# Storing attention outputs already split: a two-layer encoder trunk on one core

## The chip, the core and the metric

The kernel runs on one core of a Trainium2 chip. A core has TensorE (PE in the profile, with its weight loads as PEld), VectorE (DVE), ScalarE (ACT), GpSimd (POOL) and SyncE (SP), each with its own instruction stream, in order. SP issues all of this kernel's DMAs, on one queue that 16 DMA engines serve. The metric is device time in microseconds of one execution; before the change it is 2732.51 us, the median of 3 runs (2729.88 to 2735.3).

## The reference: what is computed

One inference step of a streaming encoder with two layers, for a prompt (1024 positions) and 8 samples of 16 positions, which stand together as 1152 rows (nine tiles of 128, the last one all samples).

```
for l in range(DEPTH):                                   # 2
    sh_m, sc_m, g_m, sh_f, sc_f, g_f = split(silu(c) @ w_ada[l] + b_ada[l], 6)
    h = x * (1 + sc_m) + sh_m
    # layer 0: window attention (128 back, 16 heads, 4 key heads, sinks, T5 bias)
    # layer 1: band attention (8 chunks of 64 back, 16 heads, clipped relative bias), shared K/V
    o = softmax(q @ k.T * 0.125 + bias) @ v
    x = layer_norm(ALPHA * x + (1 + g_m) * (o @ w_o[l]), ln_g[l, 0], ln_b[l, 0])
    f = (gelu(conv3(h2 @ w_up)[g]) * conv3(h2 @ w_up)[a]) @ w_down[l]
    x = layer_norm(ALPHA * x + (1 + g_f) * f, ln_g[l, 1], ln_b[l, 1])
```

Everything is float32. A matrix product is made with three products of halves: each operand is split into a high part (cast to the rounded format fp32r) and a low part (the rest), and hi*lo, lo*hi and hi*hi are added up. So each operand of a large product stands twice, as `hi` and `lo`, and a *split* is one cast (mostly on ScalarE, `L183`) and one subtraction (on POOL or VectorE, `L194`).

## The kernel before

The tensor `H` (128 partitions, 2 parts, 8 chunks of 128 channels, 1152 rows) holds the left operand of each projection, both parts. In attention it holds the input of the query projections; once the last query block (`qblock`, at `L313`) has read it, it is filled again with the attention outputs, which the output projection (`mmX`, `L326`) reads.

Attention goes through 8 pairs of heads `c`, each with two heads `a`, each head with two halves `h` of 512 queries; a half is two steps of the loop over `work` (64 steps). Step by step the loop issues scores (`L558`, `L561`), the row minimum with the bias (`L525`), the exponential (`L529`), transposes (`L587`) with a split of the probabilities (`L593`, `L594`), and some steps later `finish`: `values` multiplies with V (`L609`), adds the two partial results into the buffer `on` (`L622`, `L623`), and `normalise` loads the reciprocal row sums into `rb` (`L644`) and multiplies on POOL (`L647`). The biases are loaded at `L537`, two heads deep, and their corners are set by POOL (`L538`, `L539`).

`on` has room for one pair of heads. For the pairs 0 to 5 each normalised half is stored to DRAM, `oN` (`L649`). The pairs 6 and 7 are split straight into `H`. After the last query block the loop loads the stored pairs back into the low part of `H` (`oload`, `L659`, steps 51 to 55 by the table `OAT`), and casts them there: `ocast`, `L664`, steps 52 to 58 by the table `CAT`, one ScalarE cast and one POOL subtraction in place for each pair and one for the first half of the samples' outputs.

Beside this run the 16 *items*, the samples' attention (`L701`, `L727`, `L736`, `L749`, with cache loads such as `L689`), in the steps of `ITEMS`; the adaLN products of layer 0 (`L240`, weights loaded at `L232`) as background work; and the loads of the output projection's weights (`WAT`).

`out_proj` then takes the tiles in the order 8, 0, 1, ... 7. A tile's two halves go to PSUM banks 0 to 3 in turn, and VectorE evicts each by a product with the gate row (`L1122`): `gateS`, one row for each sample, for tile 8, and `gateP` for the others. These tables and the two rows of the layer norm come from `ln_consts`: four loads (`L971` gateP, `L972` gateS, `L979` twice), which the code orders behind the last load of reciprocals (`issue_after(self.lastdma)`). In the arena `F`, `gateS` has columns 6396 to 7420, which during attention belong to the samples' queries and the first score buffer.

A planner orders each engine's instructions: it runs the program in a model of the chip and takes, on each engine, the instruction that is ready there and earliest in the program.

Of the kernel before, what the change touches and what calls it, by code (L numbers as in the profile page):

```python
# [10 lines left out]
F32 = mybir.dt.float32  # L11
# [4 lines left out]
D = 1024  # L16
# [31 lines left out]
OAT = {51: (0, 1, 2), 52: (3,), 53: (4,), 54: (5,), 55: (6,)}  # L48
CAT = {52: 0, 53: 1, 54: 2, 55: 3, 56: 4, 57: 5, 58: 6}
WAT = {52: 0, 54: 1, 56: 3, 59: 2}  # L50
# [55 lines left out]
class Trunk:  # L106
    def __init__(self, ctx, tc, I, O):
# [4 lines left out]
        nc = self.nc  # L112
# [280 lines left out]
    def attention(self, l, wk):  # L393
        nc, I = self.nc, self.I
# [245 lines left out]
        def normalise(c, a, h):  # L640
            r = slice(64 * a, 64 * a + 64)
            q = slice(h * 512, h * 512 + 512)
            src = self.rD[l][2 * c + a : 2 * c + a + 1, q]
            st = nc.sync.dma_start(rb[r, :], bass.AP(src.tensor, src.offset, [[0, 64], [1, 512]]))  # L644
# [8 lines left out]
        def oview(c):  # L653
            if c < 6:
                return [self.H[:, i, c, 0:1024] for i in range(2)]
            return [self.H[:, i, 0:4, 1024:1152] for i in range(2)]

        def oload(c):
            nc.sync.dma_start(oview(c)[1].bitcast(F32), self.oN[c] if c < 6 else self.oSD.rearrange("c p t -> p c t"))  # L659
# [127 lines left out]
        def finish(k):  # L787
            x = halves[k]
            values(x)
            if x.h:  # L790
# [17 lines left out]
        for i, x in enumerate(work):  # L808
            scores(x)
            k = i // 2  # L810
# [134 lines left out]
    def ln_region(self):  # L945
# [18 lines left out]
    def ln_consts(self, l, i):  # L964
        self.ln_gates(l, i)
        self.ln_rows(l, i)

    def ln_gates(self, l, i):
        nc = self.nc
        g = self.gd[2 * l + i]  # L970
        nc.sync.dma_start(self.gateP, bass.AP(g.tensor, g.offset, [[0, 128], [1, D]]))  # L971
        nc.sync.dma_start(self.gateS, bass.AP(g.tensor, g.offset + D, [[D, 8], [0, 16], [1, D]]))  # L972

# [120 lines left out]
    def out_proj(self, l, xsrc, xdst, aff):  # L1094
# [985 lines left out]
```

## Time and profile before

| | us |
|---|---|
| median of 3 runs | 2732.51 (2729.88 to 2735.3) |
| the profiled execution | 2728.86 |
| its span in the trace | 2727.1 |
| TensorE busy | 2627.6 (96%) |
| VectorE busy | 1936.6 (71%) |
| ScalarE busy | 1346.0 (49%) |
| POOL busy | 1067.1 (39%) |
| DMA | 498.29 MB, 55.4% of 16 engines' span |

An engine's busy time is the sum of its instructions' times. In a row such as `L183 ACT CAST H<-F ... x2 | 1.2, 611 | 0.0` stand the line of the kernel, the engine, the operation, what it writes and reads, how often, then the busy us, the mean ns of one, and the engine's idle time before them. In a timeline, the first numbers are start and duration in us, and brackets tell how long the engine had been idle and what ended that. In a view of stretches the share of the DMA engines comes last but one and can be a little over 1 where packets overlap.

### The profile page before, as it was taken

To read this page: it belongs to the slowest core of one execution; us is meant where nothing else is said; L and a number is where in the kernel's file an instruction comes from. 1 tells how busy PE (TensorE), PEld (TensorE's weight loads), DVE (VectorE), ACT (ScalarE), POOL (GpSimd) and SP (SyncE) were. 2 spreads that over 40 slices of the span, in tenths; PEclk is the share of its full clock that TensorE was granted. 3 is DMA by queue.
4 is the path that set the end of the run, shared out by engine and by line. 5 is a ranking of instruction groups with operands and counts; after the bars stand their busy time and mean duration, and the time that the engine had idled before them with its cause. 6 is when DMAs were issued, how large, how long until landed. Compare 5 with 4: busy or idle time off the path is not lost. (4 is left out here: it accounts for less than half of the span.)

```text
span 2727.1 us, 47308 instructions
## 1 busy us (share of the span) xinstructions
PE 2627.6 (96%) x17394; PEld 2343.4 (86%) x17394; DVE 1936.6 (71%) x3846; ACT 1346.0 (49%) x2777; POOL 1067.1 (39%) x771
## 2 busy tenths in 40 slices
PE   7999889999999999999999999989999999999997
PEld 6997768989999998888898888867899999998786
DVE  4376768876677675767764677777888777878668
ACT  3475733533343344444446666672445454556553
POOL 3032523444344447675220121242467666552101
PEclk9999999999999999999999999999999999999999
DMA  8656534644443447666658457783444334349673
GB/s 321 207 156 197 155 110 166 219 172 140 149 149 138 152 140 240 222 224 218 232 198 279 142 151 199 197 255 131 170 153 174 139 126 146 118 145 297 220 240 124
DMA packets 229384, 498.29 MB, mean 183 GB/s; under 512 B 37440, under 2 KB 98960, under 8 KB 229152
## 3 DMA queue, kind: packets, MB, share of 16 engines
q1 hardware_dynamic: 229152, 495.27, 55.4%
q8 instruction: 137, 2.24, 0.4%
q14 instruction: 95, 0.78, 0.1%
HBM read 378.15 MB, written 126.47 MB: 185 GB/s over the span
## 5 line engine op out<-in xcount | busy, mean ns | idle before, releaser
L1237 PE MATMUL PS<-H,wh 128*128 128x256 f32 (+1 forms) x2304 | 353.8, 295 | 0.0
L1237 PEld LDWEIGHTS PS<-H,wh 128*128 128x128 f32 x2304 | 321.0, 189 | 0.0
L1197 DVE TENSOR_TENSOR F<-PS,F 128x256 f32<-128x256 f32 (+1 forms) x446 | 196.8, 451 | 159.5 <-PE PS L1237 153.4
L183 ACT CAST wh<-F 128x512 fp32r<-128x512 f32 (+3 forms) x221 | 135.5, 625 | 197.6 <-PE PS L1237 91.5
L194 DVE TENSOR_TENSOR wl<-F,wh 128x512 fp32r<-128x512 f32 (+2 forms) x205 | 198.3, 978 | 43.3 <-ACT wh L183 42.9
L1237 PE MATMUL PS<-H,wl 128*128 128x320 f32 (+1 forms) x1152 | 201.9, 296 | 4.9 <-DVE wl L194 2.6
L1237 PE MATMUL PS<-xa,wh 128*128 128x320 f32 (+1 forms) x1168 | 178.9, 294 | 0.0
L1237 PEld LDWEIGHTS PS<-H,wl 128*128 128x128 f32 x1152 | 169.2, 189 | 11.2 <-issue 5.1
L1237 PEld LDWEIGHTS PS<-xa,wh 128*128 128x128 f32 x1168 | 162.3, 189 | 0.0
L647 POOL TENSOR_TENSOR F<-F,x2r 64x512 f32<-64x512 f32 x62 | 79.2, 1278 | 208.1 <-DVE F L623 186.4
L1495 DVE TENSOR_TENSOR xa<-xa 128x384 fp32r<-128x384 f32 x66 | 100.5, 1535 | 77.5 <-ACT xa L183 64.3
L183 ACT CAST wh<-ws 128x512 fp32r<-128x512 f32 (+1 forms) x123 | 90.8, 744 | 114.5 <-PE PS L1237 49.9
L1357 POOL TENSOR_TENSOR F<-F 128x1152 f32<-128x1152 f32 x44 | 124.6, 2833 | 44.2 <-DVE F L1350 24.4
L313 PE MATMUL PS<-H,w0r 128*128 128x384 f32 (+1 forms) x720 | 137.0, 340 | 0.0
L1286 DVE SCALAR_TENSOR_TENSOR F<-F 128x1024 f32<-128x1024 f32 (+2 forms) x160 | 132.5, 878 | 4.8 <-ACT F L1325 4.0
L525 DVE CUSTOM_DVE_ANT_0 F<-PS,F,C 128x256 f32<-128x256 f32 (+3 forms) x208 | 97.2, 479 | 50.8 <-PE PS L561 25.1
L326 PE MATMUL PS<-xa,H 128*128 128x512 f32 x504 | 128.2, 395 | 5.2 <-ACT xa L183 3.3
L313 PE MATMUL PS<-H,wh 128*128 128x384 f32 (+1 forms) x672 | 132.8, 339 | 0.0
L313 PEld LDWEIGHTS PS<-H,w0r 128*128 128x128 f32 x720 | 124.6, 188 | 1.6 <-DVE F L633 0.4
L326 PE MATMUL PS<-wh,H 128*128 128x512 f32 (+1 forms) x468 | 118.0, 360 | 0.7 <-ACT wh L183 0.5
L587 PE MATMUL PS<-C,F 128*128 128x128 f32 x720 | 111.6, 279 | 6.9 <-DVE C L636 3.1
L313 PEld LDWEIGHTS PS<-H,wh 128*128 128x128 f32 x672 | 117.1, 188 | 0.5 <-issue 0.2
(361 smaller groups left out, 6917.0 us busy)
## 6 DMA issues: line engine op xcount, KB each, us to landing
ws<-in_adaw_dram SPq DMA_DIRECT2D x63, 512.0 KB
ws<-in_wup_dram SPq DMA_DIRECT2D x51, 512.0 KB
F<-in_adaw_dram SPq DMA_DIRECT2D x49, 512.0 KB
actD<-F SPq DMA_DIRECT2D x33, 576.0 KB
F<-in_wup_dram SPq DMA_DIRECT2D x37, 512.0 KB
ws<-in_wdn_dram SPq DMA_DIRECT2D x33, 512.0 KB
F<-in_wdn_dram SPq DMA_DIRECT2D x33, 512.0 KB
xa<-kH SPq DMA_DIRECT2D x60, 256.0 KB
```

What stands on the lines that cost most here:

```text
L183: nc.scalar.copy(out, in_)
L194: self.eng(el).tensor_sub(lo, src, hi.bitcast(F32))
L313: mm = self.nc.tensor.matmul(out[:, 0:n], w[a][:, k * 128 : k * 128 + 128], H[:, p, k, s0 : s0 + n], start=i == 0, stop=i == 23)
L326: self.nc.tensor.matmul(out[:, 0:n], H[:, p, j * kn + k, t0 : t0 + 128], w[a][:, k * n : k * n + n], start=i == 0, stop=i == 23,)
L525: nc.vector.tensor_tensor_reduce(out=p[:, c0 : c0 + w], in0=ps, in1=b, scale=1.0, scalar=init, op0=ALU.add, op1=ALU.min, accum_out=nm)
L587: nc.tensor.transpose(t[:, n * 128 : n * 128 + 128], p[:, (kt - k0) * 128 : (kt - k0) * 128 + 128], self.ident)
L647: self.eng("v" if last else "p").tensor_mul(on[r, q], on[r, q], rb[r, :])
L1197: nc.vector.tensor_add(d, v(ps), a if len(a.shape) == 3 else v(a))
L1237: self.pairmm = nc.tensor.matmul(ps[:, 0:m], w[a][:, k * 128 : k * 128 + 128], x(p, k, n), start=start and c == 0, stop=c == 11, skip_grou ...
L1286: nc.vector.scalar_tensor_tensor(o, u, cw[:, cc, i : i + 1], o, op0=ALU.mult, op1=ALU.add)
L1357: nc.gpsimd.tensor_mul(yg, yg, ya)
L1495: nc.vector.tensor_sub(lo, raw, hi.bitcast(F32))
```

## The change

Finished halves are no longer stored in float32 one head at a time. When both heads of a pair have a half ready, it is put on the list `parts`; the next `finish` first calls `ostore`, which splits the 128x512 block of `on` into `ohl` (ScalarE cast, POOL subtraction) and stores both parts with one DMA. `oN` becomes six blocks of two parts. `oload` then brings both parts of a pair back in one DMA, into both parts of `H`, and the casts of these six pairs go; the samples' cast stays, at step 58. `rb` moves within `X2` to make room for `ohl`. The samples' gate table gets the place of `ohl` and is loaded after the last step of the loop; `ln_gates` leaves it out for the output projection. `zt` moves to where `gateS` was in `F`.

```
-CAT = {52: 0, 53: 1, 54: 2, 55: 3, 56: 4, 57: 5, 58: 6}
+CAT = 58
...
-        self.oN = dr.tile([7, 128, 1024], F32, name="oN")
+        self.oN = dr.tile([6, 2, 128, 1024], F32, name="oN")
...
-        rb = self.X2[:, 3840:4352].bitcast(F32)
+        rb = self.X2[:, 3072:3584].bitcast(F32)
+        ohl = self.X2[:, 3584:4608].rearrange("p (i q) -> p i q", i=2)
+        self.gateS = self.X2[:, 3584:4608].bitcast(F32)
+        parts = []
...
-            if c < 6:
-                nc.sync.dma_start(self.oN[c, r, q], on[r, q])
+            if a and c < 6:
+                parts.append((c, q))
...
+        def ostore():
+            while parts:
+                c, q = parts.pop(0)
+                self.split(on[:, q], ohl[:, 0], ohl[:, 1], "a", "p")
+                nc.sync.dma_start(self.oN[c, :, :, q].rearrange("i p t -> p i t"), ohl.bitcast(F32))
+
+        def oload(c):
             if c < 6:
-                return [self.H[:, i, c, 0:1024] for i in range(2)]
-            return [self.H[:, i, 0:4, 1024:1152] for i in range(2)]
-
-        def oload(c):
-            nc.sync.dma_start(oview(c)[1].bitcast(F32), self.oN[c] if c < 6 else self.oSD.rearrange("c p t -> p c t"))
-
-        def ocast(c):
-            hi, lo = oview(c)
+                src = self.oN[c].rearrange("i p t -> p i t")
+                nc.sync.dma_start(self.H[:, :, c, 0:1024].bitcast(F32), src)
+            else:
+                nc.sync.dma_start(self.H[:, 1, 0:4, 1024:1152].bitcast(F32), self.oSD.rearrange("c p t -> p c t"))
+
+        def ocast():
+            hi, lo = [self.H[:, i, 0:4, 1024:1152] for i in range(2)]
...
         def finish(k):
             x = halves[k]
+            ostore()
             values(x)
...
-            if i in CAT:
-                ocast(CAT[i])
+            if i == CAT:
+                ocast()
...
         assert not items
+        g = self.gd[2 * l]
+        nc.sync.dma_start(self.gateS, bass.AP(g.tensor, g.offset + D, [[D, 8], [0, 16], [1, D]]))
         for f in steps:
             f()
...
-        for k in ("gateS", "gateP", "lng", "lnb"):
+        self.zt = fa.take(1024)
+        for k in ("gateP", "lng", "lnb"):
             setattr(self, k, fa.take(1024))
         y = fa.take(1152)
         self.ya = Ring([y[:, i * 384 : i * 384 + 384] for i in range(3)])
-        self.zt = fa.take(1024)
...
-    def ln_gates(self, l, i):
+    def ln_gates(self, l, i, samples=True):
...
-        nc.sync.dma_start(self.gateS, bass.AP(g.tensor, g.offset + D, [[D, 8], [0, 16], [1, D]]))
+        if samples:
+            nc.sync.dma_start(self.gateS, bass.AP(g.tensor, g.offset + D, [[D, 8], [0, 16], [1, D]]))
...
         with self.tc.issue_after(self.lastdma):
-            self.ln_consts(l, 0)
+            self.ln_gates(l, 0, False)
+            self.ln_rows(l, 0)
```

More of the change, by code (lines that the diff above doesn't have):

```diff
@@ L647, in normalise @@
             self.eng("v" if last else "p").tensor_mul(on[r, q], on[r, q], rb[r, :])
-            if c < 6:
-                nc.sync.dma_start(self.oN[c, r, q], on[r, q])
+            if a and c < 6:
+                parts.append((c, q))
             elif a:
                 self.split(on[:, q], self.H[:, 0, c, q], self.H[:, 1, c, q], "a", "v" if c == 7 else "p")
-        def oview(c):
-            if c < 6:
-                return [self.H[:, i, c, 0:1024] for i in range(2)]
-            return [self.H[:, i, 0:4, 1024:1152] for i in range(2)]
-        def oload(c):
-            nc.sync.dma_start(oview(c)[1].bitcast(F32), self.oN[c] if c < 6 else self.oSD.rearrange("c p t -> p c t"))
-        def ocast(c):
-            hi, lo = oview(c)
+        def ostore():
[4 more added lines that the diff above has]
+        def oload(c):
+            if c < 6:
+                src = self.oN[c].rearrange("i p t -> p i t")
[4 more added lines that the diff above has]
+            hi, lo = [self.H[:, i, 0:4, 1024:1152] for i in range(2)]
             with self.tc.issue_after(self.lastexp):
@@ L960, in ln_region @@
         self.ya = Ring([y[:, i * 384 : i * 384 + 384] for i in range(3)])
-        self.zt = fa.take(1024)
         assert fa.o <= self.NF, fa.o
-    def ln_consts(self, l, i):
-        self.ln_gates(l, i)
-        self.ln_rows(l, i)
-    def ln_gates(self, l, i):
+    def ln_gates(self, l, i, samples=True):
         nc = self.nc
```

## The prediction, made before the result was known

> **What bounds the kernel now.** I read the page's busy shares first, then the stretches at the end of both attention stages, then the single engines there.
>
> ```profile
> span 2727.1 us, 47308 instructions
> PE 2627.6 (96%) x17394; PEld 2343.4 (86%) x17394; DVE 1936.6 (71%) x3846; ACT 1346.0 (49%) x2777; POOL 1067.1 (39%) x771
> ```
>
> TensorE has work for 96% of the span; about 100 us are idle. An edit that moves work of the other engines changes the time only where TensorE idles. The next view cuts both attention stages into stretches (columns: busy us of PE, PEld, DVE, ACT, POOL, granted TensorE clock, share of the DMA engines, GB/s). Layer 0 attends until about 385 us, layer 1 until about 1870 us.
>
> ```profile
> 110.00:296.00 186.00, 179.85 (x1450) 155.47 (x1449) 123.91 (x422) 120.55 (x350) 50.30 (x55) 0.99 0.55 168
> 300.00:310.00 10.00, 9.61 (x91) 7.31 (x90) 8.25 (x33) 9.74 (x28) 3.69 (x3) 1.00 1.02 333
> 310.00:325.00 15.00, 10.99 (x88) 7.82 (x86) 10.10 (x39) 10.84 (x32) 13.08 (x12) 0.80 0.58 183
> 325.00:345.00 20.00, 16.78 (x156) 11.97 (x155) 17.02 (x66) 18.04 (x51) 16.10 (x13) 0.98 0.27 80
> 345.00:385.00 40.00, 32.88 (x228) 23.64 (x227) 23.52 (x62) 13.81 (x30) 8.76 (x8) 1.00 0.33 93
> 385.00:390.00 5.00, 2.81 (x13) 1.98 (x11) 0.30 (x1) 0.00 (x0) 0.00 (x0) 1.00 1.00 219
> 390.00:395.00 5.00, 4.56 (x13) 3.62 (x14) 4.93 (x9) 1.94 (x2) 0.83 (x1) 0.66 0.35 141
> ...
> 1520.00:1765.00 245.00, 235.98 (x1687) 210.78 (x1687) 177.81 (x553) 163.52 (x385) 51.18 (x53) 1.00 0.62 167
> 1775.00:1780.00 5.00, 4.50 (x36) 3.29 (x34) 4.19 (x12) 4.85 (x10) 3.65 (x2) 1.00 1.07 372
> 1775.00:1815.00 40.00, 32.66 (x272) 23.55 (x271) 28.33 (x97) 30.16 (x66) 25.06 (x18) 0.91 1.00 293
> 1805.00:1810.00 5.00, 0.28 (x8) 0.31 (x12) 2.65 (x6) 1.35 (x3) 4.92 (x4) 0.72 1.09 333
> 1810.00:1815.00 5.00, 5.00 (x45) 3.24 (x38) 2.36 (x8) 1.30 (x3) 1.09 (x3) 0.60 0.94 292
> 1815.00:1830.00 15.00, 14.67 (x148) 11.72 (x147) 14.12 (x49) 13.58 (x35) 7.33 (x7) 1.00 0.69 201
> ```
>
> The long middles are TensorE's: 179.85 of 186 us and 235.98 of 245 us. The ends are not. Layer 0 idles 0.39 + 4.01 + 3.22 = 7.6 us between 300 and 345, and layer 1 idles 40 - 32.66 = 7.3 us between 1775 and 1815. In these ends the DMA engines are full: 1.02 for 10 us in layer 0, 1.00 for 40 us in layer 1. That is where this change puts its larger loads.
>
> **The gate table.** The DVE, TensorE and SP timelines around 378 to 395 us, in that order:
>
> ```profile
> 389.70 1.29 DVE L1122 TENSOR_TENSOR F<-PS,F 128x512 f32<-128x512 f32 x2 [5.06 <-DMA F<-gd]
> ...
> 390.44 2.76 PE L326 MATMUL PS<-w0r,H 128*128 128x512 f32 x6 [2.64 <-DVE F L1122]
> 397.61 1.55 PE L326 MATMUL PS<-w0r,H 128*128 128x512 f32 x6
> ...
> 377.14 0.45 SPq L644 DMA_DIRECT2D x2r<-rD  x1
> 377.69 0.54 SPq L971 DMA_DIRECT2D F<-gd  x1
> 378.27 0.67 SPq L972 DMA_DIRECT2D F<-gd  x1
> 379.00 0.92 SPq L979 DMA_DIRECT2D F<-in_ln_dram  x2
> ```
>
> The samples' table (L972) goes out only after the last load of reciprocals (L644), together with three other 512 KB tables. The output projection does the samples' tile first, so its first eviction on VectorE waits 5.06 us for that table, and TensorE, out of banks, idles 2.64 us. Then six matmuls take 2.76 us where the same six take 1.55 us later, and the granted clock of 390 to 395 us is 0.66: 5 x 0.34 = 1.7 us more. With the table loaded at the end of the loop, some 30 us earlier, into a place that no other late work holds, the wait for it goes. The prompt's table (L971) is issued ahead of it today and is needed one tile later, so what is late next is VectorE itself. Gain: 2.64 + 1.7 = 4.3 us, with the bounds 2.6 (no clock) and 5.06 (all of VectorE's wait). In layer 1 no row shows a wait for this table: gain 0. Its own transfer falls on 345 to 385 us at a DMA share of 0.33, and cover is plentiful; were it gone, the 512 KB would cost 1.4 us (at 372 GB/s, below).
>
> [...]
>
> **The late casts that go.** From the groups of ScalarE and POOL between 1765 and 1830 us (layer 0 has the same seven of each), and the nearest rows of the casts that come:
>
> ```profile
> L183 ACT CAST H<-H 128x1024 fp32r<-128x1024 f32 (+1 forms) x7 | 6.8, 973 | 0.0
> L194 POOL TENSOR_TENSOR H<-H 128x1024 fp32r<-128x1024 f32 (+1 forms) x7 | 15.4, 2212 | 4.3 <-ACT H L183 3.9 <-PE PS L635 0.3
> ...
> L183 ACT CAST H<-F 128x512 fp32r<-128x512 f32 x2 | 1.2, 611 | 0.0
> 344.76 1.31 POOL L194 TENSOR_TENSOR H<-F,H 128x512 fp32r<-128x512 f32 x1 [0.84 <-ACT H L183]
> ```
>
> Six of each seven go (the seventh is the samples' and stays): about 6 us of ScalarE and 14 us of POOL per layer. POOL is off the path there. ScalarE matters where it is full beside an idle TensorE: 9.74 of 10 us in 300 to 310 (TensorE idle 0.39) and 18.04 of 20 in 325 to 345 (idle 3.22). In layer 1 it is at 30.16 of 40 and the idle time belongs to a load (below). Bounds: 0 and 0.39 + 3.22 = 3.6 us. I take 2.0, a little over half, since the exponentials that stand behind these casts also wait for VectorE (17.02 of 20).
>
> **The casts that come.** Twelve per layer, one for each finished half of a pair of heads: 12 x 0.61 = 7.3 us of ScalarE and 12 x 1.31 = 15.7 us of POOL, spread over 186 and 245 us in which ScalarE is at 65 to 67% and POOL at 21 to 27%. TensorE's work covers them; without that cover they would cost up to 7.3 us a layer. The middles' idle time is 6.2 and 9.0 us already, so a few exponentials delayed by 0.6 us will show: bounds 0 and 3, taken 1.0 for both layers. Behind a waiting cast on ScalarE stand the exponentials, and for these waits TensorE.
>
> **Stores and loads.** Today's issues by line, for both layers (the last row has first and last start): stores of 128 KB, 24 a layer, and loads of 512 KB, 6 a layer.
>
> ```profile
> oN<-F SPq DMA_DIRECT2D x48, 128.0 KB
> H<-oN SPq DMA_DIRECT2D x12, 512.0 KB
> F<-gd SPq DMA_DIRECT2D x8, 512.0 KB
> L659 SPq DMA_DIRECT2D H<-oN x12: 319/382/535, 296.9 to 1787.7; - x12
> ```
>
> The stores become 12 a layer of 512 KB, so 3 MB more; over 186 us at a share of 0.55 they are hidden, and SP issues 12 fewer. The loads stay 6 a layer at the same steps, but carry both parts: 1 MB each, 3.1 MB more, in the full stretch. How a queued load costs today shows in these rows (SP's issues, the chain of waits, TensorE's timeline):
>
> ```profile
> 1770.17 2.25 SPq L659 DMA_DIRECT2D H<-oN  x5
> 1802.37 7.22 DMA F<-in_cvB_dram
> 1809.72 1.67 PE L736 MATMUL PS<-F,C 128*32 128x128 f32 x24 [4.75 <-DMA F<-in_cvB_dram]
> 1982.29 3.71 DMA F<-hD
> ...
> 304.54 0.35 SPq L232 DMA_DIRECT2D ws<-in_adaw_dram  x1
> 311.74 0.64 PE L240 MATMUL PS<-ws,C 128*32 128x256 f32 x8 [1.39 <-DMA ws<-in_adaw_dram]
> 1769.81 2.42 PE L313 MATMUL PS<-H,wh 128*128 128x384 f32 x13
> ```
>
> A 512 KB load takes 3.71 us in a quiet place (F<-hD) and 7.22 us behind others (a sample's values, L736's), so 3.5 us of queue cost TensorE 4.75 us, plus a clock of 0.72 and 0.60. In layer 0 the adaLN weights, issued at 304.54, are awaited at 311.74, with no slack. The new bytes: 524,288 B / 372 GB/s (the best 5 us above) = 1.41 us a load, so 8.5 us for six; at the mean of 293 GB/s they are 10.7. The loads also start later: today the first overwrites only the low part of H and goes at 1770.17, while the last group of matmuls that reads the high part (L313) runs until 1769.81 + 2.42 = 1772.2; from now on it has to wait for these, 2.0 us. So what queues behind (keys, biases, sample caches, reciprocals, adaLN weights) lands up to 10 us later until the DMA has idle time: 15 x 0.42 = 6.3 us of it in 310 to 325, 15 x 0.31 = 4.7 us in 1815 to 1830.
>
> Bounds for TensorE: 0 if consumers are placed later and other matmuls fill in; in full 8.5 us in layer 1 and 7 us in layer 0 (five loads of 1.41, as the sixth comes after the queue has emptied). Of the two places known, one passed on more than its queue time (4.75 of 3.5) and one 1.39; dozens of other loads in those stretches passed on none. I take half: 4.3 + 3.5 = 7.8 us. Both ends stay in the range.
>
> **Sum**, against the profiled execution (2728.86 us with a span of 2727.1): -4.3 - 2.0 + 1.0 + 7.8 = +2.5, so 2731.4. It stood 3.65 us under the median of 2732.51; on the median the forecast is 2735.0. Its own range, with a quarter to three quarters of the loads' price, is 2731 to 2739.
>
> **Rivals.** (1) The backlog is paid in full and the kernel is slower. One mechanism: in both ends the DMA engines are full, transfers on the one queue are served in their order of issue, and TensorE, in order too, stands at L240 and L736 as at 311.74 and 1809.72. It decides once consumers have under 7 us of slack. Price 15.5 in place of 7.8: +10.2, 2742.7. Against it: a stall of TensorE also holds back later issues, so the queue empties meanwhile.
>
> [...]
>
> (2) The loads are hidden: the order of work shifts the consumers, as for the dozens of loads that nobody waits for. Price 0: -5.3, 2727.2. Against it: two waits at zero slack already stand there.
>
> (3) POOL holds up the new casts. It waits for biases with everything behind it:
>
> ```profile
> 241.64 0.14 POOL L538 MEMSET F<- 64x64 f32 x1 [10.32 <-DMA F<-ska]
> ```
>
> The next half's ScalarE copy into the same buffer must now wait for POOL's subtraction within one half, 186 us / 23 = 8 us, where the single product could be late by four halves before. A wait of 10.32 us would pass on 2.2 us; twice or so in each layer makes some +4 in place of +1: 2738 to 2739. For it: the buffer is single. Against: most such waits are under 8 us.
>
> (4) The early table does not help, because the prompt's table or VectorE is late at the same place: the 4.3 us stay, 2739.3. Against: L971 is issued ahead of L972 and used a tile later.
>
> **Chances.** The forecast 0.44; (1) 0.20; (2) 0.27; (3) 0.05; (4) 0.04. This kernel's measurement can tell about 0.2%, 5.5 us, from no change. Under 2727.0 lies most of (2), taken down by its remaining unknowns to 0.20, and 0.01 of the rest: faster 0.21. Over 2738.0 lie all of (1), the upper fifth of the forecast (0.08) and most of (3) and (4) (0.06): slower 0.34. Between them: 0.45. Range: all gains at their best and no cost for the loads is -5.06 - 3.6 = -8.7, 2723.8; the smallest gains, 3 for the casts and 15.5 for the loads is +15.9, 2748.4, which I cut to 2747 as all at once is unlikely: 2724 to 2747.
>
> **What would show it.** Gate: L1122's wait for F<-gd is gone and the clock between 385 and 395 is 1.00. Casts: no H<-H groups of 128x1024; 24 casts of 128x512 from F in the middles, whose idle time stays under 6.2 + 9.0 + 3 us. Loads: oN of 1 MB after the last L313; DMA share 1.00 until about 320 and 1823; stalls at L240 and L736 longer by half the backlog. Idle time of 300 to 345 and 1775 to 1830 below today's would prove me wrong towards (2), more than 8 us above it towards (1); waits of ScalarE's L622 for POOL towards (3).

## The result, and the profile after

The changed kernel takes 2757.65 us (median of 5 runs, 2751.08 to 2760.04), the kernel before 2729.88 us on the same chip (5 runs): a ratio of 1.0099, with a 95% interval of 1.0085 to 1.0112. It is **slower by about 27 us**, and above the whole predicted range. The profiled execution took 2754.03 us. Its page begins:

```profile
span 2752.2 us, 47303 instructions
PE 2639.9 (96%) x17394; PEld 2352.9 (85%) x17394; DVE 1928.8 (70%) x3846; ACT 1349.1 (49%) x2789; POOL 1067.2 (39%) x783
```

The span grew by 25.1 us. TensorE's busy time grew by 12.3 us although its 17394 matmuls are the same, so about half of the loss is not waiting but matmuls at a lower clock (0.984 over the span, 0.991 before). The stretches that answer to those of before (columns as there):

```profile
300.00:310.00 10.00, 8.64 (x79) 6.35 (x78) 8.60 (x31) 9.54 (x27) 2.38 (x1) 1.00 0.89 348
310.00:325.00 15.00, 11.50 (x93) 7.83 (x93) 9.80 (x37) 8.89 (x30) 4.30 (x6) 0.89 0.90 297
325.00:345.00 20.00, 15.13 (x130) 11.07 (x126) 13.58 (x54) 10.54 (x32) 10.84 (x13) 0.83 0.67 190
345.00:385.00 40.00, 32.60 (x214) 22.32 (x215) 21.56 (x74) 15.58 (x44) 6.32 (x5) 0.87 0.21 66
395.00:400.00 5.00, 5.00 (x23) 4.09 (x22) 3.35 (x5) 0.72 (x1) 0.00 (x0) 1.00 0.79 287
1785.00:1825.00 40.00, 29.57 (x228) 22.07 (x226) 25.91 (x86) 24.32 (x59) 9.53 (x9) 0.91 1.07 314
1825.00:1840.00 15.00, 10.17 (x75) 7.56 (x75) 6.83 (x26) 4.91 (x13) 1.98 (x4) 0.77 1.01 253
```

The full stretch of the DMA engines now reaches from 1785 to 1840 us, 55 us where it was 40. To compare the same work in all kernels, I cut both ends by counting matmuls: layer 0's end from the 2150th to the 2850th of the trace, layer 1's from the 11600th to the 12240th. Before, then after:

```profile
287.30:402.20 114.90, 97.48 (x701) 74.06 (x700) 78.84 (x245) 61.67 (x159) 50.02 (x40) 0.96 0.44 133
1775.90:1864.00 88.10, 79.14 (x642) 59.27 (x641) 61.10 (x201) 57.43 (x133) 36.22 (x31) 0.96 0.71 209
```

```profile
287.80:409.20 121.40, 102.25 (x702) 76.39 (x701) 79.59 (x249) 58.63 (x157) 38.42 (x37) 0.92 0.50 160
1785.60:1888.40 102.80, 84.47 (x642) 63.20 (x641) 62.99 (x201) 53.17 (x127) 23.11 (x26) 0.90 0.78 219
```

Layer 0's end is 6.5 us longer: idle time (length less PE busy) 17.42 to 19.15, so +1.7, and busy time +4.8 at a clock of 0.92 in place of 0.96. Layer 1's end is 14.7 us longer: idle 8.96 to 18.33, +9.4, and busy +5.3 at 0.90 in place of 0.96. Together these are 21.2 of the 25.1 us.

**Where TensorE stops in layer 1.** SP's issues (the first in layer 0), then TensorE, VectorE, and pieces of the chain of waits, all of after:

```profile
333.77 0.68 SPq L846 DMA_DIRECT2D x2r<-gd  x1
...
1781.22 2.94 SPq L665 DMA_DIRECT2D H<-oN  x5
...
1812.22 0.63 SPq L846 DMA_DIRECT2D x2r<-gd  x1
```

```profile
1828.38 1.11 PE L590 MATMUL PS<-C,F 128*128 128x128 f32 x4 [5.45 <-DVE C L639]
```

```profile
1828.05 0.28 DVE L639 COPY C<-PS 4x128 f32<-4x128 f32 x1 [4.37 <-DMA rD<-C]
```

```profile
1813.45 13.63 DMA F<-in_ckB_dram
1827.10 7.01 DMA wl<-kH
1834.17 5.40 DMA F<-in_cvB_dram
```

Five 1 MB loads leave within 3 us. The gate table (`L846`) leaves at 1812.22, in the middle of the full stretch: the planner issued it right behind the last pair's load, once `ohl` was free, and not at the end of the loop (in layer 0 at 333.77). What is issued behind them lands late: a sample's keys 13.63 us after the issue, and the 2 KB store of reciprocals so late that VectorE's next copy into its one buffer (`L639`) waits 4.37 us and TensorE 5.45 us.

**What a stop costs twice.** Stretches of after, in pairs: some 5 us in which TensorE has little to do, and the 6 to 7 us that follow.

```profile
342.00:348.00 6.00, 2.33 (x21) 1.64 (x21) 3.05 (x9) 3.13 (x10) 0.57 (x1) 0.97 0.24 79
348.00:354.00 6.00, 6.00 (x49) 3.94 (x49) 4.99 (x20) 4.21 (x14) 3.80 (x3) 0.50 0.32 109
1820.50:1825.50 5.00, 1.54 (x11) 0.89 (x9) 2.35 (x4) 2.08 (x4) 0.31 (x1) 1.00 1.11 219
1825.50:1832.50 7.00, 3.98 (x27) 2.91 (x27) 4.27 (x15) 2.12 (x6) 1.27 (x1) 0.51 0.93 216
1793.50:1798.50 5.00, 1.74 (x13) 1.02 (x11) 3.17 (x5) 2.69 (x5) 0.00 (x0) 0.99 1.09 356
1798.50:1804.50 6.00, 5.17 (x26) 4.17 (x30) 4.49 (x17) 1.91 (x5) 0.00 (x0) 0.50 1.07 264
```

In these three pairs TensorE was busy for 31 to 39% of the first stretch, and the granted clock was 0.50 to 0.51 in the one behind it: by estimate some 3 us more for each (6 to 7 us at half clock), if TensorE works through it. The first of these stretches has no long gap; TensorE's two longest there:

```profile
345.84 0.55 PE L590 MATMUL PS<-C,F 128*128 128x128 f32 x3 [1.86 <-DVE F L639]
347.75 1.11 PE L590 MATMUL PS<-C,F 128*128 128x128 f32 x4 [1.36 <-DVE F L737]
```

Several short gaps make up the 3.67 us of idle time there. By after's clock records this half clock lasted from 347.70 to 354.53 us, 6.83 us, as did each of the two others above. In the 3.40 us before it TensorE had 0.55 us of work:

```profile
344.30:347.70 3.40, 0.55 (x3) 0.31 (x3) 1.90 (x5) 2.65 (x7) 0.00 (x0) 1.00 0.11 39
```

From 100 to 2650 us the records of before and after have 20 stretches of half clock, 12 of 3.41 us and 8 of 6.83. I divided both traces into steps of 3.41 us, at whose ends all these changes lie. Half clock followed all 15 steps at full clock in which TensorE was busy for under 40%, 3 of 4 with 40 to 50%, 2 of 23 with 50 to 70%, and none of the 1422 above that. Each of the 20 stretches ended behind a step with 92% or more.

**The gate's own stall** is gone, as predicted: VectorE's first eviction of the samples' tile waits for nothing, and the clock of 395 to 400 us is 1.00.

```profile
396.10 0.69 DVE L1131 TENSOR_TENSOR F<-PS,x2r 128x512 f32<-128x512 f32 x1
```

### The profile page after: what moved, and what is told of

The parts are those of the page before. It is cut to its first block, busy times and chain, and to the rows that moved or that the text cites. A ratio compares the mean times of both kernels' runs of the same rounds, so it can differ in the third digit from the quotient of the medians.

```text
span 2752.2 us, 47303 instructions
## 1 busy us (share of the span) xinstructions
PE 2639.9 (96%) x17394; PEld 2352.9 (85%) x17394; DVE 1928.8 (70%) x3846; ACT 1349.1 (49%) x2789; POOL 1067.2 (39%) x783
## 4 chain that ended last, share of the span: by engine, by line
PE 32%; DVE 6%; DMA 6%; ACT 2%; issue 2%; POOL 1%; SPq 1%; DVEq 0%; ACTq 0%; POOLq 0%
PE PS L1246 13%; PE PS L1636 6%; PE PS L313 4%; PE PS L326 4%; PE PS L612 2%; PE PS L590 1%; DVE wl L194 1%; PE PS L561 1%; DMA F<-hmD 1%; PE PS L564 1%; DMA xa<-actD 1%; ACT F L949 1%; DMA F<-in_wdn_dram 1%; DMA F<-in_ckB_dram 0%; DVE xa L194 0%
## 5 line engine op out<-in xcount | busy, mean ns | idle before, releaser
L1504 DVE TENSOR_TENSOR xa<-xa 128x384 fp32r<-128x384 f32 x66 | 93.8, 1430 | 87.7 <-ACT xa L183 87.6
L1366 POOL TENSOR_TENSOR F<-F 128x1152 f32<-128x1152 f32 x44 | 124.6, 2832 | 43.9 <-DVE F L1359 23.1
L590 PE MATMUL PS<-C,F 128*128 128x128 f32 x720 | 114.7, 281 | 20.6 <-DVE C L639 11.1
```

Of the source, the lines that this page charges most:

```text
L590: nc.tensor.transpose(t[:, n * 128 : n * 128 + 128], p[:, (kt - k0) * 128 : (kt - k0) * 128 + 128], self.ident)
L1366: nc.gpsimd.tensor_mul(yg, yg, ya)
L1504: nc.vector.tensor_sub(lo, raw, hi.bitcast(F32))
```

## The experiments

Each of e1 to e18 was timed beside the kernel before on one chip, but not all on the same one; the ratios are compared. The ends are the two counted stretches of its trace, in us. Layer 1's end repeats well: 88.1 to 89.9 in before, e5, e15 to e18 and e1. Layer 0's does not: e15 and e17, which differ only in how one table is loaded, have 105.7 and 113.8, so a difference there means little below some 8 us. Some of these kernels compute less than the reference: e4, e5 and e16 leave out the low part of six of eight chunks, e12 and e14 the six late loads of each layer.

| kernel | what | ratio to before (95% interval) | layer 0's end | layer 1's end |
|---|---|---|---|---|
| before | | 1 | 114.9 | 88.1 |
| after | | 1.0099 (1.0085 to 1.0112) | 121.4 | 102.8 |
| e1 | before + early table | 1.0007 (0.9993 to 1.0020) | 113.9 | 89.4 |
| e2 | after, old table | 1.0058 (1.0043 to 1.0072) | 114.3 | 98.3 |
| e3 | after, table held | 1.0083 (1.0068 to 1.0097) | 119.9 | 104.6 |
| e4 | after, 512 KB loads | 1.0046 (1.0028 to 1.0063) | 110.4 | 95.8 |
| e5 | after, 512 KB loads, old table | 1.0019 (1.0006 to 1.0032) | 116.3 | 88.7 |
| e6 | after, table in eight loads | 1.0091 (1.0072 to 1.0110) | 124.0 | 102.1 |
| e7 | after, two reciprocal buffers | 1.0106 (1.0088 to 1.0125) | 117.8 | 110.7 |
| e8 | before + loads twice | 1.0053 (1.0034 to 1.0072) | 125.6 | 99.1 |
| e9 | e2, loads held apart | 1.0046 (1.0033 to 1.0059) | 116.1 | 99.6 |
| e10 | after, old table in layer 1 | 1.0062 (1.0048 to 1.0076) | 121.9 | 95.7 |
| e11 | before, loads apart, table early in layer 0 | 1.0003 (0.9993 to 1.0014) | 108.6 | 95.5 |
| e12 | e2 without the loads | 1.0015 (1.0006 to 1.0024) | 116.1 | 92.9 |
| e13 | before + splits and stores | 1.0057 (1.0035 to 1.0079) | 115.3 | 91.9 |
| e14 | before without late loads and casts | 1.0006 (0.9992 to 1.0019) | 113.9 | 92.0 |
| e15 | e11 in layer 0, before in layer 1 | 0.9986 (0.9971 to 1.0001) | 105.7 | 89.0 |
| e16 | e5, two buffers for the splits | 0.9993 (0.9978 to 1.0008) | 112.2 | 89.5 |
| e17 | e15, table in eight loads | 1.0004 (0.9991 to 1.0018) | 113.8 | 89.5 |
| e18 | before, loads apart in layer 0 | 0.9990 (0.9974 to 1.0006) | 112.3 | 89.9 |

### Four corners: the loads and the table apart (e1, e2, e4, e5)

e1: the table's move alone, on the kernel before. e2: the change without the table's move.

```diff
 # e1, on before
+        self.gateS = self.X2[:, 3584:4608].bitcast(F32)      # rb moves to 3072
         assert not items
+        nc.sync.dma_start(self.gateS, ...)
 # e2, on after
         assert not items
-        nc.sync.dma_start(self.gateS, ...)                    # back in ln_gates, behind lastdma
```

> The kernel before with only the gate table's part of the change: table in X2, loaded by the loop's end, no split stores, no larger loads, all late casts kept. In this kernel nothing else needs that place, so the load goes out in the quiet middle of each attention stage and not in its full end. Theory A (the larger loads make the loss, the table's move is a gain): 4.45 us faster than before, the gap that closed in the two traces, about 2725.4; the 2.64 us gap of TensorE at the output projection is gone, the ends 300 to 345 and 1775 to 1830 us as before. Theory B (the table's transfer itself costs as much as it saves wherever it stands): no change, within 2 us of before.

> The kernel after with the gate table loaded where the kernel before loads it, behind the last reciprocals, into its old place; split stores and larger loads kept. Theory A (larger loads alone fill the queue): the losses of +10 at layer 0's end and +15 at layer 1's end stay, the 4.45 us stall returns: 2762, so 32 us over before. Theory B (the table, issued at 333.8 and 1812.2 us in the full queue, makes a good part of it): the +4.5 us after 342 us in layer 0 and at least 5 us of layer 1's 1815 to 1830 us go, the stall returns: 2750 to 2753.

e4: the high part alone is loaded. e5: e4 with e2's table.

```diff
-                nc.sync.dma_start(self.H[:, :, c, 0:1024].bitcast(F32), src)
+                nc.sync.dma_start(self.H[:, 0, c, 0:1024].bitcast(F32), self.oN[c, 0])
```

> The kernel after, but each of the six late loads brings only the high part (512 KB, as before), so the low part of six of eight chunks is left out of the output projection's input; splits, stores of 512 KB, gate table as after. Theory A (bytes of the larger loads): the ends return to those of before or better, since the late casts are gone too: 2724 to 2730, so 0 to 5 us faster than before. Theory B (the table in the queue): about half of the loss stays, 2738 to 2745. Theory C (a later start of the loads, since they must wait until the high part of H is free, or the planner's new order of work): most of the loss stays, 2748 to 2757.

> The fourth corner: the kernel after with the loads of 512 KB (high part only, the low part of six of eight chunks is left out) and the gate table in its old place and at its old time. Of the loss of 27 us, the old gate took away 11 (e2) and the small loads 14 (e4). Theory D (two separate prices, the bytes of the loads and the early table, which add): 27 - 11 - 14, so 0 to 5 us over before, 2730 to 2735. Theory E (both are prices of the split stores or of the planner's new order, which each edit only shifts): 8 us or more over before, as e4.

On 2730 us the ratios are +1.9 (e1), +15.8 (e2), +12.6 (e4), +5.2 (e5) and +27.0 us (after). So the larger loads cost 15.8 - 5.2 = **10.6 us**, the early table 12.6 - 5.2 = **7.3 us** net of the stall that it takes away, and what both leave is **5.2 us**; the sum of 23.1 leaves 3.9 us to their acting together, which the intervals don't tell from nothing. Each single ratio is uncertain by 3.5 to 5 us, and each of these differences by 5 us or more. (e2 came out below both of its forecasts, e4 as theory B had it.) Layer 1's end says where: 88.7 us with neither, 98.3 with the loads, 95.8 with the table, 102.8 with both. These are e5's, e2's and e4's rows of it:

```profile
1782.20:1870.90 88.70, 80.39 (x643) 60.80 (x642) 62.11 (x202) 53.37 (x128) 23.23 (x26) 0.96 0.75 220
```

```profile
1775.20:1873.50 98.30, 82.48 (x642) 61.26 (x641) 62.06 (x201) 53.48 (x128) 23.96 (x26) 0.93 0.78 233
```

```profile
1773.70:1869.50 95.80, 81.82 (x641) 60.44 (x641) 60.82 (x202) 53.84 (x128) 24.19 (x26) 0.93 0.72 201
```

The loads' 9.6 us in layer 1 (e2 less e5) are 7.5 us idle and 2.1 us clock; beside the early table (after less e4) they are 7.0. In layer 0's end the loads don't show: 114.3 us with them (e2), 116.3 without (e5). Theory D (two prices that add) holds best; A alone and B alone fall, each explains half.

e1 is the surprise of the four. Its first eviction waits for nothing either, so the stall is gone:

```profile
389.79 0.69 DVE L1123 TENSOR_TENSOR F<-PS,x2r 128x512 f32<-128x512 f32 x1
```

Yet it is not 4.45 us faster; its interval ends at 1.9 us faster. Its load left at 189.22 and 1511.85 us, in the middles, so e1 prices the table in a quiet place and not in the tail's queue. Its layer-0 end:

```profile
289.00:402.90 113.90, 99.97 (x701) 75.90 (x701) 77.84 (x245) 62.03 (x159) 51.30 (x40) 0.93 0.40 130
```

Idle time fell by 3.5 us (17.42 to 13.93), but busy time rose by 2.5 us (97.48 to 99.97) at a clock of 0.93 for 0.96. A stall that was removed was worth less than its length here; which thin stretches lowered the clock in its place, and whether they do so in every execution, the runs don't tell.

### The large loads on the kernel before (e8), apart (e9), and none (e12, e14)

```diff
 # e8, on before
-        nc.sync.dma_start(oview(c)[1].bitcast(F32), self.oN[c])
+        for i in (0, 1):
+            nc.sync.dma_start(oview(c)[i].bitcast(F32), self.oN[c])
 # e9, on e2: one load behind each half's store of reciprocals
-OAT = {51: (0, 1, 2), 52: (3,), 53: (4,), 54: (5,), 55: (6,)}
+OAT = {51: (0,), 53: (1,), 55: (2, 6), 57: (3,), 59: (4,), 61: (5,)}
-                oload(c)
+                with self.tc.issue_after(self.rdst):
+                    oload(c)
```

> The kernel before, with each of its six late 512 KB loads followed by a second one of the same data into the high part of H, which the late cast then overwrites as before: 3.1 MB more at the same place of the queue, no split stores, no early table, all casts kept. Theory A (bytes and late start of the larger loads): 10 to 16 us over before, 2741 to 2747, nearly all of it between 1785 and 1830 us and 300 and 345 us. Theory E (the planner's order or the split stores): within 4 us of before.

> The kernel of split stores, 1 MB loads and the old gate (e2, 16 us over before), with the six loads held apart: each goes out only after the reciprocals' store of another half of a pair of heads, about 8 us apart, instead of five in 3 us. The bytes are the same. Theory J (the bunch is the price: ten microseconds of queue at once make TensorE stop, and the clock with it): layer 1's end falls from 10.2 us over before to 0 to 3, the whole to 2733 to 2737. Theory K (the bytes are the price wherever they go in the full stretch): 2740 to 2745.

e8 is 0.53% slower, 14.5 us, without split stores, early table or changed casts: **the added bytes are enough** (theory A). The later start that comes with them is not the cause in layer 1: e5's loads also wait for the high part of `H`, and its end there is that of before (88.7 us). e9 keeps 0.46% of e2's 0.58%, and layer 1's end stays at 99.6 us (theory K, at its upper end). Held apart, the loads move the stop to other places; TensorE in e9:

```profile
1815.71 1.66 PE L743 MATMUL PS<-F,C 128*32 128x128 f32 x24 [4.26 <-DMA F<-in_cvB_dram]
...
1855.15 0.99 PE L743 MATMUL PS<-F,C 128*32 128x128 f32 x24 [3.32 <-DMA F<-in_cvB_dram]
```

Whether the bunch has a price of its own stays open: holding the loads apart lengthens layer 1's end by 7 us with the 512 KB loads of before too (e11, below), which may hide in e9 what it wins.

e12 and e14 leave the six loads out altogether, on the side of after and of before.

```diff
 # e12, on e2
-            if c < 6:
-                src = self.oN[c].rearrange("i p t -> p i t")
-                nc.sync.dma_start(self.H[:, :, c, 0:1024].bitcast(F32), src)
-            else:
+            if c == 6:
 # e14, on before
-            if i in CAT:
+            if CAT.get(i) == 6:
-                oload(c)
+                if c == 6:
+                    oload(c)
```

> The floor: split stores and the old gate, but the six late loads are left out altogether, so the output projection computes with what stands in H for six of eight chunks. If the loads' bytes are the price (e2 16 us, with half of the bytes e5 5 us over before): a straight line through these gives 5 us under before, 2725; the DMA share of 1775 to 1815 falls from 1.00 to some 0.7. If the tail is bound by the sample caches anyway: 2730 to 2735, as e5.

> The kernel before without its six late loads and six late casts a layer (the output projection then computes with what stands in H for six of eight chunks); stores and gate as before. It gives the most that any change to these loads and casts can win. Prediction's terms (casts 2 us, loads' bytes at the price that e2 minus e5 gives, 10.6 us for 6.2 MB over both layers, if the price is a straight line): 8 to 12 us under before, 2719 to 2723. If only bytes beyond what the queue can carry cost (a bend, not a line): 0 to 4 us under before, 2727 to 2731.

e14: 1.0006 (0.9992 to 1.0019). Six loads and six casts a layer less, and nothing is won that shows (at most 2.2 us); layer 1's end is even 92.0 us. e12 is 4.1 us over before. So the price has **a bend**: 0 MB +4.1, 3.1 MB a layer +5.2, 6.3 MB +15.8 us (e12, e5, e2), and on the side of before +1.6, 0 and +14.5 us (e14, before, e8). Within the intervals the 512 KB loads of before were free and the second half of the bytes was not; of the late casts no price shows.

### The table: held, in pieces, in one layer (e3, e6, e10)

```diff
 # e3: issued behind the load of reciprocals of pair 7's first half
-        nc.sync.dma_start(self.gateS, ...)
+        with self.tc.issue_after(self.rd70):
+            nc.sync.dma_start(self.gateS, ...)
 # e6
+        for s in range(8):
+            nc.sync.dma_start(self.gateS[16 * s : 16 * s + 16], ...)        # row s, 16 times
 # e10: at the loop's end for l == 0 only; layer 1 in ln_gates, behind lastdma
```

> The kernel after, whole, but the gate table's load is held until the load of the reciprocals of the seventh head pair's next-to-last half, about 348 us in layer 0 and 1855 us in layer 1, when the queue is empty again. Theory A: 2757, as after. Theory B: the early table's price goes and its gain stays: 2745 to 2749; the gap of 1.86 us at 345.84 and that of 5.45 us at 1828.38 (values waiting for the reciprocals' copy on VectorE) are under 1 us.

> The kernel after with the gate table loaded at the same place by eight loads of 16 rows (64 KB each) in place of one of 128 rows. In the traces the one load moves its 512 KB in about 7 us at half of the DMA engines' share, where other loads of 512 KB take 1.4 us of all of them. Theory F (the table is dear because its one transfer keeps half of the engines for 7 us, and what queues behind it waits): with eight loads spread over all engines most of the table's 11 us goes, 2742 to 2748, less some 3 us of issue time on SP. Theory G (its price is its place in a full queue, whatever its shape): 2755 to 2760.

> The kernel after, whole, but in layer 1 the gate table is loaded behind the last reciprocals again (where before never waited for it); in layer 0 it stays at the loop's end. By the corners (layer 1's end: 0.5 us over before with neither, 10.2 with the loads alone, 7.7 with the table alone, 14.7 with both) the table in layer 1 is 4.5 to 7 us of pure loss: 2750 to 2753, with layer 1's end at 8 to 11 us over before and layer 0's as after. If the table's price there was chance: 2755 to 2760.

e10 is about as expected of a price in layer 1: 1.0062, and its end falls from 102.8 to 95.7 us; by e5 and e4 it is 7.1 us as well, by e2 and after 4.5. Holding the table back did not help (e3, 1.0083): it went out at 1843.57 in layer 1, and now the samples' values that were issued behind it were late. e3's TensorE, and a stretch:

```profile
1860.21 1.66 PE L746 MATMUL PS<-F,C 128*32 128x128 f32 x24 [4.06 <-DMA F<-in_cvB_dram]
```

```profile
1859.00:1865.00 6.00, 4.79 (x38) 2.71 (x39) 3.48 (x11) 2.12 (x5) 1.27 (x1) 0.51 0.43 132
```

The table's load is a slow one. In before, it moves almost alone from 1859 to 1865 us:

```profile
1859.00:1865.00 6.00, 5.36 (x25) 3.61 (x24) 2.23 (x5) 1.93 (x4) 0.32 (x1) 1.00 0.37 90
```

540 KB (6 us at 90 GB/s) at a share of 0.37 of the engines' time, four times the 1.41 us on which I had put it; the share is 0.50 from 1862 to 1863 us, where the load moves. But theory F falls: e6, with its eight loads of 16 rows, is no faster (1.0091; layer 1's end 102.1). In place of one issue come eight on SP, in layer 0 in the way of the other loads:

```profile
335.09 5.72 SPq L847 DMA_DIRECT2D x2r<-gd  x8
```

So in layer 1 the table costs by standing in the tail's queue at all, whatever its shape (G); behind the tail it costs nothing that shows (e10).

### The buffer at which TensorE stopped (e7)

```diff
-            nc.vector.tensor_copy(rl[0:4, :], t[0:4, 0:128])
+            rr = rl[64 * x.h : 64 * x.h + 4, :]
+            nc.vector.tensor_copy(rr, t[0:4, 0:128])
```

> The kernel after, but the reciprocals are copied to one of two buffers in turn (other partitions of the same tile), so that VectorE's copy does not wait for the store of the half before it. Theory H (the delay in the full queue reaches TensorE through this one buffer: 1.86 us at 345.84 and 5.45 us at 1828.38, with the copies behind): 2745 to 2752. Theory I (the load of the reciprocals, keys and caches behind the same queue are as late, so TensorE stops at the next of them): 2754 to 2760.

1.0106: no gain (theory I). VectorE no longer waits for the store, and TensorE stops 5 to 8 us at the next late loads instead:

```profile
1828.62 1.13 PE L710 MATMUL PS<-F 128*32 128x272 f32 x8 [5.38 <-DMA F<-kS]
1840.55 1.66 PE L745 MATMUL PS<-F,C 128*32 128x128 f32 x24 [8.09 <-DMA F<-in_cvB_dram]
```

The row that ended a stall named where the delay came out, not its cause. (The edit also changed the planner's order, so that the 8 us by which its layer-1 end is longer than after's are not a price of the buffer.)

### The front half: splits and stores (e13, e16)

```diff
 # e13, on before: ostore() as in after, into a table that nobody reads; old stores stay
 # e16, on e5
-        pts = [(x2.take(512), x2.take(512)) for _ in range(3)]
+        pts = [(x2.take(512), x2.take(512)) for _ in range(2)]
+        ohls = Ring([... for o in (3584, 2048)])             # ohl = ohls.next() in ostore
```

> The kernel before with the new front half added and nothing taken away: each finished half is also split on ScalarE and POOL and the two parts are stored (512 KB, twelve a layer, into a table that nobody reads); the old stores, 512 KB loads, late casts and the old gate stay. Theory L (the front half has a price of its own, which is why e5 and e12, with few or no late bytes, are still 5 and 4 us over before): 3 to 6 us over before, 2733 to 2737, in the middles and in the ends. If it is free, and the 4 to 5 us come from the changed order of work without the late casts: within 2 us of before.

> The corner with small loads and the old gate (e5, 0.19% over before), with two buffers in turn for the split halves; the second takes one of the six places of the transposed probabilities. In after's trace the split's cast on ScalarE waits three times in layer 0's middle, 6.0 us in all, until the store of the half before has left the one buffer, with exponentials and copies behind it. Theory M (this wait is the front half's price): it is gone from the waits, the 2.48 us gap of TensorE at 184 us too, and the kernel stands within 3 us of before, 2728 to 2732. If the price is the two engines' extra work: as e5, 5 us over before. The lost place may cost 1 to 2 us in either case.

e13 is 0.57% slower, 15.6 us with an interval from 9.6 to 21.6, above both forecasts: the front half is not free. Here it comes on top of the old stores, which after no longer has. In e13's trace its casts wait 8.8 us from 110 to 300 us, and TensorE 2.31 us behind one of them:

```profile
L184 ACT CAST x2r<-F 128x512 fp32r<-128x512 f32 x10 | 6.2, 617 | 8.8 <-DMA oP<-x2r 6.4 <-POOL F L650 2.4
```

The same shows in after's middle of layer 0, in ScalarE's group of the new casts, ScalarE's and VectorE's timelines, and TensorE's:

```profile
L183 ACT CAST x2r<-F 128x512 fp32r<-128x512 f32 x10 | 6.1, 611 | 6.0 <-DMA oN<-x2r 6.0
```

```profile
177.37 0.62 ACT L183 CAST x2r<-F 128x512 fp32r<-128x512 f32 x1 [2.69 <-DMA oN<-x2r]
```

```profile
179.37 0.42 DVE L515 SCALAR_TENSOR_TENSOR xa<-PS,xa 64x256 fp32r<-64x256 f32 x1 [3.40 <-ACT xa L514]
```

```profile
180.83 0.27 PE L638 MATMUL PS<-C,F 128*4 128x128 f32 x1 [1.81 <-DVE x2r L597]
```

A cast into `ohl` may not start until the store of the half before has left it. So ScalarE stood 2.69 us at the head of its queue with exponentials and copies behind, VectorE 3.40 us, TensorE 1.81 us. In e5 the same place costs TensorE 2.48 us. With two buffers (e16) the waits for the store are gone from ScalarE's list in 110 to 300 us, and so is TensorE's gap. But the same casts now wait 4.5 us for POOL's product, where they waited 5.4 us for the store in e5:

```profile
L183 ACT CAST x2r<-F 128x512 fp32r<-128x512 f32 x10 | 6.2, 616 | 4.5 <-POOL F L649 4.5
```

The kernel stands at 0.9993 (0.9978 to 1.0008) where e5 stands at 1.0019 (1.0006 to 1.0032): 7.1 us by the middles, though the two intervals overlap by a hair and come from two chips. The traces show less of it: idle time of 110 to 300 us is 9.7 us in e5 and 7.2 us in e16, and the profiled executions took 2731.78 and 2732.14 us. Theory M, that **the wait rather than the work is the front half's price**, is the likelier, but is not shown.

### Tries at a faster kernel (e11, e15, e17, e18)

The loads of before held apart as in e9, casts two steps behind, the table early in layer 0 (e11); the same in layer 0 only (e15); then with eight loads for the table (e17), and without the table's move (e18).

```diff
+            for c in (OAT, OA1)[l].get(i, ()):               # OA1: the table of before, for layer 1
+                with self.tc.issue_after(self.rdst):         # layer 0 only
+                    oload(c)
```

> A try at a version better than both: the kernel before with its 512 KB loads held apart as in e9 and each late cast two steps after its load, and the gate table loaded early in layer 0 alone. If the bunch of loads already costs before (5 of them in 2.3 us at 1770, 9 us of idle TensorE and 3.5 us of slow clock in layer 1's end) and J holds: 4 to 10 us faster than before, 2720 to 2726. If casts that come later delay the output projection, or K holds: within 4 us of before.

> A second try at a version better than both: layer 0 as in e11 (512 KB loads held apart, casts two steps later, gate table early; its layer-0 end was 6.3 us shorter than before's in the trace), layer 1 as in before (in e11 its end was 7.4 us longer). If both ends carry over: 4 to 7 us faster than before, 2724 to 2727. If e11's layer 0 was chance: within 2 us of before.

> The second try (e15, ratio 0.9986, interval 0.9971 to 1.0001) with layer 0's early table brought by eight loads of 16 rows over all DMA engines, so that the adaLN weights behind it in the middle are not late (e1's trace lost 2.4 us there). If e15's gain is real: 5 to 9 us faster than before, 2721 to 2726, and the middle of layer 0 within 1 us of before. If it was chance: within 3 us of before.

> The kernel before with only layer 0's six loads held apart and their casts later; the gate table stays in its old place, so the 2.64 us gap at the output projection returns. If e15's layer-0 end (9.3 us shorter in the trace) is the table's doing alone (4.4 us of gap and clock, the rest chance): within 2 us of before. If it is the loads' doing: 4 to 6 us faster, 2725 to 2728.

e11 made layer 1's end 7 us longer (95.5), as e9's held loads had, probably because loads that come later stand before the last samples' values. e15 looked like 4 us, but its interval reaches 1.0001, and e17 (1.0004) and e18 (0.9990, to 1.0006) do not repeat it. No version that beats before is shown.

## Why the prediction was wrong

The forecast was +2.5 us and the measured change +27.0. Of the 24.5 us between them, by the corners, the gate table makes 11.6 (-4.3 forecast, +7.3 measured), the two terms of the casts with all else that the corners leave 6.2 (-1.0 and +5.2), the larger loads 2.8 (7.8 and 10.6), and 3.9 the corners don't part. So three steps failed; the table's is the largest, and it had not only the size but the sign wrong.

**"I take half: 4.3 + 3.5 = 7.8 us"**, the larger loads, was too small, and rival (1), "the backlog is paid in full", was its direction. Its order of service stands in the trace of before: the five loads issued from 1770.17 to 1772.03 us landed in the order of their issue, the first 3.58 us and the last 7.29 us after it. Measured: 10.6 us by the corners, 14.5 us on the kernel before. In layer 1 alone it was 7.0 to 9.6 us in place of 4.3, about the upper bound of 8.5, which counted only idle time; the 3.5 us for layer 0 don't show. The places were wrong too: no wait at L240 stands in after's layer-0 end, and at L736 (now `L744`) none for its values' load. TensorE stopped at the transposes (`L590`) instead, 8.7 us in three waits for the copy of the reciprocals. The stop of 5.45 us was paid a second time as clock (0.51 from 1825.50 to 1832.50 us); I had counted that for the gate's stall (1.7 us) and not for the loads' stalls, though the rows beside L736 (0.72 and 0.60) showed it there too. In the whole, 10.1 of 21.2 us in the two ends are clock (4.8 + 5.3). "A stall of TensorE also holds back later issues, so the queue empties meanwhile" did not save it: the share stays over 1.0 until 1840 us.

**"Its own transfer falls on 345 to 385 us at a DMA share of 0.33, and cover is plentiful"** and "in layer 1 ... gain 0" are the step that cost most. The planner issued the table at 333.77 and 1812.22 us, when its place came free, not where the code has it; in layer 1 that is the full stretch, and the 1.4 us for its bytes stand against 4.5 to 7.1 us. The gain in layer 0 was right in kind: stall and slow clock behind it are gone. Its 4.3 us are not confirmed in the total (e1: at most 1.9 us faster).

**The new casts, "+1.0"**, were put at their work and at delayed exponentials of 0.6 us each. What the traces show is a wait: the cast for the store that still reads the one `ohl`. Rival (3) looked for a wait of ScalarE's copy for POOL; none stands in after's two middles, one of 2.2 us in layer 0's end, and I never asked what frees `ohl`. The corners leave 5.2 us (e5), over my bound of 3; how much of it this wait makes is open, as TensorE's gap behind it is 1.8 to 2.5 us.

**The late casts, "-2.0"**, are not seen: without them and without the loads e14 wins nothing that shows, at most 2.2 us.

The middles of after, for the marks set there:

```profile
110.00:296.00 186.00, 177.41 (x1439) 152.75 (x1437) 121.77 (x419) 122.74 (x357) 63.12 (x64) 1.00 0.57 180
1520.00:1765.00 245.00, 236.27 (x1667) 211.75 (x1666) 177.65 (x549) 169.66 (x397) 63.42 (x67) 1.00 0.65 179
```

Layer 0's idles 8.6 us in place of 6.2, and 1.8 of these 2.4 us are the gap behind the cast's wait; layer 1's 8.7 in place of 9.0, as predicted. Right were also that the loads of before are hidden as rival (2) had it (true for 512 KB, false for 1 MB), and the marks for the gate. The mark for idle time pointed to rival (1), barely: 300 to 345 us rose by 2.1 us (7.6 to 9.7) and 1775 to 1830 by 6.1 (7.7 to 13.8), together just over the 8 us set there. It was blunt, as it left out the clock, which in 325 to 345 fell from 0.98 to 0.83.

What stays open: which part makes layer 0's end longer. With large loads and the early table it is 117.8 to 124.0 us in five kernels (after, e3, e6, e7, e10), with one of the two 110.4 to 125.6 (e1, e2, e4, e8, e9), with the early table and 512 KB loads held apart 105.7 to 113.8 (e11, e15, e17). Its length hangs also on how many steps of half clock fall into it: the mean clock is 0.98 in the shortest (e15) and 0.85 in the longest (e8). The 3.9 us by which the corners don't add up may be that.

## What to carry to other kernels

When the DMA engines are full in a stretch, price a load there by what is issued behind it, not by its bytes alone, and add the clock for each stop of TensorE: here 3.1 MB more in each layer cost 10.6 us, by the ends nearly all of it in layer 1, where the 3.1 MB already there were free, and clock was 10.1 of the 21.2 us by which the two ends of after grew. Under a planner like this one a load goes out when its buffer comes free (here at 1812.22 us, in the full stretch), not where the code has it, so look up that time before calling its cover plentiful. When a new step stands between a compute engine and a DMA, ask what frees its buffer: with one buffer, ScalarE waited here 2.69 us for a transfer at the head of its queue.

## What the runs showed that I had not expected

In after the clock fell to 0.50 without any long gap, behind 6 us with 2.33 us of work and gaps of at most 1.86 us. In all 15 cases of before and after in which TensorE at full clock was busy for under 40% of a step of 3.41 us, half clock followed.

One DMA issue on SP lasted as long as a load in the full stretch (7.22 us in before). Behind the five 1 MB loads the issue of one small load of the samples' values lasted 7.63 us; before it took 0.79 us at the same place. After, then before:

```profile
304.56 7.63 SPq L685 DMA_DIRECT2D F<-vS  x1
312.28 0.38 SPq L232 DMA_DIRECT2D ws<-in_adaw_dram  x1
```

```profile
303.62 0.79 SPq L677 DMA_DIRECT2D F<-vS  x1
```

It came again in all five other kernels with five 1 MB loads in a bunch (e2, e3, e6, e7 and e10: 7.49 to 7.74), and was 0.62 to 1.45 us with 512 KB loads (e5, e4), 1.45 us with loads held apart (e9) and 2.96 us with twice as many loads of 512 KB (e8). The adaLN weights, the next issue, left at 312.28 in place of 304.54 us. In layer 1 three of the five issues behind the loads, to three different places, are long too, where before they took 0.37, 0.54 and 0.61 us, so part of what landed late there had also left late:

```profile
1785.05 3.28 SPq L492 DMA_DIRECT2D xa<-vH  x1
1788.42 5.02 SPq L641 DMA_DIRECT2D rD<-C  x1
1793.96 3.60 SPq L692 DMA_DIRECT2D F<-kS  x1
```

What SP waited for there is not shown.

The load of the samples' gate table, 8 rows spread over 128 partitions, moved at a share of 0.37 of the DMA engines' time and at 90 GB/s over 6 us in before, and at a share of 0.50 from 1862 to 1863 us.
